# A hybrid encoder's feed-forward entry: differences by ScalarE and accumulating transfers, plain gates ahead of the second value block

## The chip, the core and the metric

One core of one Trainium2 chip runs the whole program. The metric is device time in microseconds (us) from the start of the program to its end; lower is better. Engines by the profile's names: PE (matrix products) and PEld (its weight loads), DVE (VectorE), ACT (ScalarE), POOL (GpSimd), SP (SyncE, which here only issues transfers).

## What is computed

Two layers of a streaming encoder over 656 token columns (528 of a prompt, 8 streams of 16). Each layer has an input projection, three head groups, an output projection, and then the gated feed-forward part that the change touches:

```python
h2 = rmsnorm(x, p['g_ffn'])
gate, val = jnp.split(h2 @ p['w_up'].astype(x.dtype), 2, axis=-1)
gate_c, ffn_new = causal_dwconv(gate, ffn_past, p['ffn_conv_w'], p['ffn_conv_b'])
x = x + (jax.nn.gelu(gate_c) * val) @ p['w_down'].astype(x.dtype)
```

Model width is 1024 (8 blocks of 128 rows), feed-forward width 2816: 22 gate blocks and 22 value blocks of 128. `causal_dwconv` is three taps along the columns; its state `ffn_past` fills two columns ahead of each stream.

## The kernel before

**Layout.** Activations lie transposed: 128 channels on the partitions, 656 columns along them. Each product is made three times from a rounded high part and a low remainder (`mm3`: hi times hi, hi times lo, lo times hi), so every weight and activation block is first split: ACT casts the high part (`whi`, `hi_h`, `fh`), DVE subtracts it for the low part (`wlo`, `lo_h`, `fh` again). The weight parts live in a ring of `NW = 4` buffers ("passing" ones, tiles whi and wlo, each half a block's depth), or, with `own=True`, in slots of their own (tiles ghi and glo).

**The feed-forward entry** is the stretch from the end of the output projection to the first Strassen products; there is one per layer (from about 397.8 and 1222.4 us). In order on PE: one group of products `e_u` for gates 0 and 1 and value 0 (`gemm_group`), value block 1 (`d_v`: two column halves, eight blocks deep, three products each, so 48), gate blocks 2 and 3 (`d_g`, 48 each; `NPG = 2`), then all remaining gate and value blocks in pairs by Strassen's seven products (`strassen`), each four blocks deep and one column half wide, so 12 instructions of PE; the first such products are value pair 0's (`d_v<-fh`).

**Right factors.** The Strassen products need seven combinations of the normalised input, which `factors` makes. It scales the eight x blocks (DVE, L1068), makes the differences t1 to t4 of halves on POOL (L1076, L1077, L1084, L1085: 16 subtractions of 128x328 in a layer), and splits each of the 7 x 4 results (ACT cast and DVE subtraction, L1090, tile fh). It is a generator with seven steps; step n needs `src[k][n]`. `FE = 2` steps are taken before the gates, the rest after.

**A plain gate** (`plain_gate`): `gate_in` puts the past columns into the tile gp by POOL (L1100, L1102), DVE evicts the products into gp with the norm's factor r (L1248), `gate_out` copies the new state into gout (POOL, L1107, L1108), then the taps run: ACT the first (L1112), DVE two more (L1115), ACT the gelu (L1118, after a table load). For value blocks 0 and 1, POOL multiplies the gate by r (L1257, L1258) and DVE multiplies the value product by it (gv, L1262 to L1264).

**What sets the order.** The program is written as one stream; each engine takes its instructions in the order printed below, and waits for others by semaphores. A DMA that POOL issues occupies POOL in that order. Weights come by SP's queue. Sums of Strassen's weight blocks are POOL's too (wcb, L985). Strassen's results are added up by DVE (L1018, L1022) as soon as each product is done, and the down projection (`d_dn`) begins once the first value pair is gated (POOL L1299) and split (hi_g, lo_g).

Of the kernel before, what the change touches and what calls it, by code (L numbers as in the profile page):

```python
# [13 lines left out]
ALU = mybir.AluOpType  # L14
# [23 lines left out]
NPG = 2  # L38
# [121 lines left out]
def trunk_kernel(ctx: ExitStack, tc: tile.TileContext, i: dict, o: dict, depth: int = 2):  # L160
# [12 lines left out]
    V, A, G, PE = nc.vector, nc.scalar, nc.gpsimd, nc.tensor  # L173

    def S(name, dt=F32):
        return slots.tile([128, T], dt, tag="S", name=name)
# [22 lines left out]
    xs = [S(f"x{m}") for m in range(8)]  # L199
# [25 lines left out]
    def par(name, k):  # L225
        c = COLS[name][0] + k
        return cst[:, c:c + 1]
# [136 lines left out]
    def w_load(w, k0, kt, parts=None):  # L364
        raw = wraw.tile([128, 8, 128], F32, tag="raw", name="raw")
        for a, b in parts or ((0, kt),):
            nc.sync.dma_start(out=raw[:, a:b], in_=w[:, (k0 + a) * 128:(k0 + b) * 128].rearrange("p (k n) -> p k n", n=128))
        return raw
# [4 lines left out]
    def w_split(raw, kt, a=0, own=False):  # L373

        half = 4 if kt in (4, 8) else 3
        units = []
        while a < kt:
            n = min(half, kt - a)
            if own:
                hi, lo = unit_s("ghi"), unit_s("glo")  # L380
            else:
                hi = wsp.tile([128, 4, 128], F32R, tag="whi", name="whi")
                lo = wsp.tile([128, 4, 128], F32R, tag="wlo", name="wlo")
            seq(A.copy(hi[:, :n], raw[:, a:a + n]))  # L384
            seq(V.tensor_tensor(out=lo[:, :n], in0=raw[:, a:a + n], in1=hi[:, :n].bitcast(F32), op=ALU.subtract))  # L385
            units += [(hi, lo, m) for m in range(n)]
            a += n
        return units

    def weights(w, k0, kt, own=False):  # L390
        return w_split(w_load(w, k0, kt), kt, 0, own)
# [8 lines left out]
    def gemm1(units, ks, rhs, nm, ab, P=PD):  # L400
        ps = P(f"d_{nm}")
        for k in range(len(ks)):
            mm3(ps, units[k], rhs[ks[k]], ab, k == 0, k == len(ks) - 1)
        return ps

    def gemm(units, ks, rhs, nm, cc=CA, P=PD):

        return [gemm1(units, ks, rhs, f"{c}_{nm}", cc[c], P) for c in range(2)]
# [652 lines left out]
    def factors(l, r, cc):  # L1061

        (a0, a1), (b0, b1) = cc
        w = a1 - a0
        src = []
        for k in range(4):
            for m in (k, k + 4):
                V.scalar_tensor_tensor(out=xs[m][:, a0:T], in0=xs[m][:, a0:T], scalar=par("g_ffn", 8 * l + m),  # L1068
                                       in1=r[:, a0:T], op0=ALU.mult, op1=ALU.mult)
            b11, b12 = xs[k][:, a0:a1], xs[k][:, b0:b1]  # L1070
            b21, b22 = xs[k + 4][:, a0:a1], xs[k + 4][:, b0:b1]
            t = S(f"ft{l}{k}")
            t1, t3 = t[:, :w], t[:, HC:HC + w]
            t = S(f"fu{l}{k}")
            t2, t4 = t[:, :w], t[:, HC:HC + w]
            G.tensor_tensor(out=t1, in0=b12, in1=b11, op=ALU.subtract)  # L1076
            G.tensor_tensor(out=t2, in0=b22, in1=t1, op=ALU.subtract)  # L1077
            src.append((b11, b21, t2, t3, t4, t1, b22))
        out = [[] for k in range(4)]
        for n in range(7):  # L1080
            for k in range(4):
                b11, b21, t2, t3, t4, t1, b22 = src[k]
                if n == 1:
                    G.tensor_tensor(out=t3, in0=b22, in1=xs[k][:, b0:b1], op=ALU.subtract)  # L1084
                    G.tensor_tensor(out=t4, in0=b21, in1=t2, op=ALU.subtract)  # L1085
                x = src[k][n]
                t = S(f"fh{l}{k}{n}", F32R)
                hi, lo = t[:, :w], t[:, HC:HC + w]
                A.copy(hi, x)
                V.tensor_tensor(out=lo, in0=x, in1=hi.bitcast(F32), op=ALU.subtract)  # L1090
                out[k].append((hi, lo))
            yield out
# [4 lines left out]
    def gate_in(l, ft, gpast, a0):  # L1097
        g = SE(f"gp{l}{ft}")
        if a0 == 0:
            G.memset(g[:, 0:2], 0.0)  # L1100
        gs = by_stream(g[:, 2 + TP:])
        G.tensor_copy(gs[:, :, 0:2], by_stream(gpast[:, ft]))  # L1102
        return g, gs
# [25 lines left out]
    def gate_dst(g, gs, cc):  # L1129
        (c0, c1), (d0, d1) = cc  # L1130
        n0 = TP - d0
        return [[(g[:, 2 + c0:2 + c1], 0, c1 - c0, same)],
                [(g[:, 2 + d0:2 + TP], 0, n0, same), (gs[:, :, 2:18], n0, n0 + 128, by_stream)]]


    ks8 = list(range(8))
    for l in range(depth):
# [7 lines left out]
        if l == 0:  # L1145
            hs = []
# [56 lines left out]
        cx, cy = (CB, CC) if l == depth - 1 else (CA, CA)  # L1203
# [19 lines left out]
        hs = []  # L1223
        wu = i["w_up"][l]
# [12 lines left out]
        wd = i["w_down"][l]  # L1237
        a0, cw = cy[0][0], cx[0][1] - cx[0][0]
        gates, vals, gts = {}, {}, {}
        fac = factors(l, r, cx)  # L1240
        for n in range(FE):
            tm = next(fac)

        def plain_gate(ft, ps):
            g, gs_ = gate_in(l, ft, gpast, a0)
            for c, dd in enumerate(gate_dst(g, gs_, cx)):
                for out, a, b, v in dd:
                    V.tensor_tensor(out=out, in0=v(ps[c][:, a:b]), in1=v(r[:, cx[c][0] + a:cx[c][0] + b]), op=ALU.mult)  # L1248
            gates[ft] = gate_out(l, ft, g, gs_, gout, a0)

        for ft in range(2):
            plain_gate(ft, ps3[ft])
        wg = [weights(wu[ft], 0, 8, True) for ft in range(2, 2 + NPG)]
        for ft in range(2):
            ps = ps3[2] if ft == 0 else gemm(weights(wu[NFF + 1], 0, 8), ks8, hs, f"v{l}1", cx, PB)
            a, av = gates.pop(ft)
# [6 lines left out]
            V.tensor_tensor(out=v[:, d0:TP], in0=ps[1][:, :n0], in1=a[:, d0:TP], op=ALU.mult)  # L1263
            V.tensor_tensor(out=by_stream(v[:, TP:T]), in0=by_stream(ps[1][:, n0:n0 + 128]), in1=av, op=ALU.mult)  # L1264

        for ft in range(2, 2 + NPG):
            plain_gate(ft, gemm(wg[ft - 2], ks8, hs, f"g{l}{ft}", cx))
        for tm in fac:
            pass

# [81 lines left out]
        for p in range(1, NFF // 2):  # L1352
            for up in (up_gate, up_val)[1 if p == 1 else 0:]:
                for st in up(p):
# [3 lines left out]
                    while due and due[0][0] <= nprod:  # L1358
                        _, n, j = due.pop(0)
# [33 lines left out]
        if l < depth - 1:  # L1393
            hs = []
# [95 lines left out]
```

## Time and profile before

| | before |
|---|---|
| time, median of 3 runs | 1680.81 us (1680.68 to 1682.55) |
| the profiled execution's own time | 1678.91 us |
| its span, first to last instruction | 1677.1 us |
| mean granted TensorE clock | 0.993 |
| PE, PEld busy | 1618.5 us (97%), 1527.1 us (91%) |
| DVE, ACT, POOL busy | 1245.9 us (74%), 879.1 us (52%), 566.8 us (34%) |
| transfers | 180.56 MB, mean 108 GB/s; POOL's queue 12672 packets, 29.37 MB |

The profiled execution ran 1.81 us outside its span and stands 1.90 us under the median of the runs. Busy times are sums over the span; the stretches that matter here are read below by windows and by single rows.

### The profile page before, as it was taken

The numbers are of one execution on the slowest core, as the hardware profiler recorded it, in microseconds if no ns is written. First come the engines' busy times: TensorE is split into PE (matmuls) and PEld (weight loads), VectorE is DVE, ScalarE is ACT, GpSimd is POOL, SyncE is SP. The second block draws the span as 40 slices with busy tenths as digits, with TensorE's granted clock in tenths as the row PEclk, the third lists the DMA queues.
The fourth block names the chain that finished last, engine by engine and source line by source line (L and its number), as shares of the span: only waits on it lengthen the run. The fifth ranks groups of instructions, "written<-read, shape, count | busy, mean of one in ns | idle before, by whom it ended". The sixth has DMA issues, their size and how long they took to land.

```text
span 1677.1 us, 28733 instructions
## 1 busy us (share of the span) xinstructions
PE 1618.5 (97%) x10774; PEld 1527.1 (91%) x10774; DVE 1245.9 (74%) x2391; ACT 879.1 (52%) x1744; POOL 566.8 (34%) x652
## 2 busy tenths in 40 slices
PE   7999999999899999999999999999999999999997
PEld 7898888898899999999998988888988899999997
DVE  6579985769987767666647898856899777777556
ACT  6656576543554444444437556566545444444444
POOL 0102220007556555554001032100276545554420
PEclk9999999999999999999999999999999999999999
DMA  6236441342144444444532364313511344444453
GB/s 226 74 95 160 111 105 36 113 136 99 45 119 102 102 106 106 105 106 112 190 103 81 95 149 98 99 56 130 179 39 51 98 105 102 102 106 99 108 136 122
DMA packets 75003, 180.56 MB, mean 108 GB/s; under 512 B 12752, under 2 KB 18384, under 8 KB 74864
## 3 DMA queue, kind: packets, MB, share of 16 engines
q1 hardware_dynamic: 62192, 149.36, 27.6%
q0 software_dynamic: 12672, 29.37, 11.2%
q8 instruction: 84, 1.38, 0.3%
q14 instruction: 55, 0.45, 0.1%
HBM read 129.80 MB, written 35.46 MB: 99 GB/s over the span
## 4 chain that ended last, share of the span: by engine, by line
PE 78%; DVE 11%; issue 4%; POOL 3%; ACT 2%; DMA 1%; SPq 0%; POOLq 0%; DVEq 0%; ACTq 0%
PE d_dn L398 16%; PE d_i L398 16%; PE d_v L398 12%; PE d_g L398 12%; PE d_oa L398 5%; PE sc L515 2%; PE e_i L398 1%; PE hl L809 1%; PE po L551 1%; DVE fh L1090 1%; DVE wlo L385 1%; PE d_fin L398 1%; PE e_u L398 1%; DVE wlo L992 1%; POOL gv L1299 1%
## 5 line engine op out<-in xcount | busy, mean ns | idle before, releaser
L398 PE MATMUL d_v<-fh,whi 128*128 128x328 f32 (+1 forms) x1120 | 251.8, 312 | 1.6 <-ACT whi L991 1.6
L384 ACT CAST whi<-raw 128x384 fp32r<-128x384 f32 (+2 forms) x243 | 132.6, 548 | 208.8 <-PE d_i L398 76.5
L398 PE MATMUL d_g<-fh,whi 128*128 128x328 f32 (+1 forms) x1008 | 226.5, 312 | 0.3 <-ACT whi L991 0.3
L398 PE MATMUL d_i<-hi_h,whi 128*128 128x328 f32 x672 | 219.3, 326 | 0.0
L398 PE MATMUL d_i<-lo_h,whi 128*128 128x328 f32 x672 | 213.9, 318 | 0.0
L398 PE MATMUL d_i<-hi_h,wlo 128*128 128x328 f32 x672 | 212.9, 317 | 0.0
L398 PE MATMUL d_dn<-hi_g,wlo 128*128 128x328 f32 (+1 forms) x640 | 199.8, 312 | 2.8 <-DVE wlo L385 2.8
L398 PE MATMUL d_dn<-hi_g,whi 128*128 128x328 f32 (+1 forms) x640 | 200.2, 313 | 1.9 <-ACT hi_g L356 1.7
L398 PE MATMUL d_dn<-lo_g,whi 128*128 128x328 f32 (+1 forms) x640 | 200.1, 313 | 1.8 <-DVE lo_g L357 1.8
L385 DVE TENSOR_TENSOR wlo<-raw,whi 128x384 fp32r<-128x384 f32 (+2 forms) x243 | 170.9, 717 | 30.5 <-ACT whi L384 22.7
L398 PEld LDWEIGHTS d_v<-fh,whi 128*128 128x128 f32 x1120 | 189.3, 189 | 2.2 <-ACT whi L991 2.2
L992 DVE TENSOR_TENSOR wlo<-wcb,whi 128x512 fp32r<-128x512 f32 x152 | 131.9, 868 | 74.9 <-ACT whi L991 72.3
L398 PE MATMUL d_v<-fh,wlo 128*128 128x328 f32 (+1 forms) x560 | 175.5, 313 | 3.3 <-DVE wlo L992 3.3
L398 PEld LDWEIGHTS d_g<-fh,whi 128*128 128x128 f32 x1008 | 170.4, 189 | 0.5 <-ACT whi L991 0.5
L398 PE MATMUL d_g<-fh,wlo 128*128 128x328 f32 (+1 forms) x504 | 157.8, 313 | 2.3 <-DVE wlo L992 2.3
L985 POOL TENSOR_TENSOR wcb<-raw 128x512 f32<-128x512 f32 x76 | 109.6, 1442 | 127.8 <-DMA raw<-in_w_up 80.2
L992 DVE TENSOR_TENSOR wlo<-raw,whi 128x512 fp32r<-128x512 f32 x114 | 114.8, 1008 | 50.7 <-ACT whi L991 50.5
L991 ACT CAST whi<-wcb 128x512 fp32r<-128x512 f32 x152 | 93.7, 620 | 110.6 <-PE d_g L398 33.3
L398 PEld LDWEIGHTS d_i<-hi_h,whi 128*128 128x128 f32 x672 | 127.5, 190 | 10.1 <-issue 5.6
L398 PEld LDWEIGHTS d_i<-lo_h,whi 128*128 128x128 f32 x672 | 127.6, 190 | 3.8 <-issue 1.3
L398 PEld LDWEIGHTS d_i<-hi_h,wlo 128*128 128x128 f32 x672 | 127.2, 189 | 3.0 <-issue 1.3
L398 PEld LDWEIGHTS d_dn<-hi_g,wlo 128*128 128x128 f32 x640 | 121.1, 189 | 3.5 <-DVE wlo L385 3.5
(394 smaller groups left out, 4026.9 us busy)
## 6 DMA issues: line engine op xcount, KB each, us to landing
raw<-in_w_up SPq DMA_DIRECT2D x88, 512.0 KB, 3.7
raw<-in_w_in SPq DMA_DIRECT2D x45, 512.0 KB, 3.7
raw<-in_w_down SPq DMA_DIRECT2D x48, 384.0 KB, 3.8
x_scr<-x SPq DMA_DIRECT2D x24, 328.0 KB, 3.2
x_scr<-dd POOLq DMA_DIRECT2D x24, 328.0 KB, 4.5
x<-x_scr SPq DMA_DIRECT2D x24, 328.0 KB, 4.4
x_scr<-dd POOLq DMA_DIRECT2D x24, 320.0 KB, 4.6
cvb<-cvt POOLq DMA_DIRECT2D x20, 328.0 KB, 5.0
```

What stands on the lines that cost most here:

```text
L384: seq(A.copy(hi[:, :n], raw[:, a:a + n]))
L385: seq(V.tensor_tensor(out=lo[:, :n], in0=raw[:, a:a + n], in1=hi[:, :n].bitcast(F32), op=ALU.subtract))
L398: PE.matmul(ps[:, :b - a], lhsT=ww[:, n], rhs=r[:, a:b], start=first and j == 0, stop=last and j == 2)
L515: PE.matmul(ps[:, o0:o0 + w], lhsT=q[64 * c:64 * c + 64, q0:q0 + 128], rhs=k[64 * c:64 * c + 64, n * w:(n + 1) * w], start=True, stop=True)
L551: PE.matmul(po[:, :128], lhsT=vt[:, j * 128:(j + 1) * 128], rhs=aT[:, j * 128:(j + 1) * 128], start=j == 0, stop=False)
L809: PE.matmul(ps[:, c * 128:(c + 1) * 128], lhsT=kk[:, 16 + 128 * c:144 + 128 * c], rhs=both(m0 + 64 * c, 64), start=True, stop=True)
L985: G.tensor_tensor(out=t, in0=x, in1=y, op=op)
L991: A.copy(hi, x)
L992: V.tensor_tensor(out=lo, in0=x, in1=hi.bitcast(F32), op=ALU.subtract)
L1090: V.tensor_tensor(out=lo, in0=x, in1=hi.bitcast(F32), op=ALU.subtract)
L1299: G.tensor_tensor(out=v[:, a0:TP], in0=v[:, a0:TP], in1=a[:, a0:TP], op=ALU.mult)
```

## The change

In `factors`, POOL's 16 subtractions of a layer go. For each k, ACT now writes four starting values: t3 = -b12 and t1 = -b11 (L1077, L1079), t2 = b11 (L1081), t4 = -b22 (L1082). POOL issues transfers that add to what lies at their destination: t3 += b22 (L1078), t1 += b12 (L1080), and in the new loop (L1086) t4 += b21, t2 += t3, t4 += t1. That is 16 ACT instructions and 20 transfers of 128x328 numbers (164 KB) in a layer. In the layer's code, the weights of gates 2 and 3 are loaded and split before `factors`, in the passing buffers and not in slots of their own, and both gates run before value block 1, with one step of `factors` taken ahead of each. The four casts and four subtractions of these weights now lie among the splits at the output projection's end; SP issues the same loads, the gates' one place earlier.

```diff
--- before.py
+++ after.py
@@ -1073,16 +1073,21 @@
             t1, t3 = t[:, :w], t[:, HC:HC + w]
             t = S(f"fu{l}{k}")
             t2, t4 = t[:, :w], t[:, HC:HC + w]
-            G.tensor_tensor(out=t1, in0=b12, in1=b11, op=ALU.subtract)
-            G.tensor_tensor(out=t2, in0=b22, in1=t1, op=ALU.subtract)
+
+            A.mul(t3, b12, -1.0)
+            G.dma_start(out=t3, in_=b22, accum_op=ALU.add)
+            A.mul(t1, b11, -1.0)
+            G.dma_start(out=t1, in_=b12, accum_op=ALU.add)
+            A.copy(t2, b11)
+            A.mul(t4, b22, -1.0)
             src.append((b11, b21, t2, t3, t4, t1, b22))
+        for n, m in ((4, 1), (2, 3), (4, 5)):
+            for s in src:
+                G.dma_start(out=s[n], in_=s[m], accum_op=ALU.add)
         out = [[] for k in range(4)]
         for n in range(7):
             for k in range(4):
                 b11, b21, t2, t3, t4, t1, b22 = src[k]
-                if n == 1:
-                    G.tensor_tensor(out=t3, in0=b22, in1=xs[k][:, b0:b1], op=ALU.subtract)
-                    G.tensor_tensor(out=t4, in0=b21, in1=t2, op=ALU.subtract)
                 x = src[k][n]
                 t = S(f"fh{l}{k}{n}", F32R)
                 hi, lo = t[:, :w], t[:, HC:HC + w]
@@ -1237,6 +1242,7 @@
         wd = i["w_down"][l]
         a0, cw = cy[0][0], cx[0][1] - cx[0][0]
         gates, vals, gts = {}, {}, {}
+        wg = [weights(wu[ft], 0, 8) for ft in range(2, 2 + NPG)]
         fac = factors(l, r, cx)
         for n in range(FE):
             tm = next(fac)
@@ -1250,7 +1256,9 @@
 
         for ft in range(2):
             plain_gate(ft, ps3[ft])
-        wg = [weights(wu[ft], 0, 8, True) for ft in range(2, 2 + NPG)]
+        for ft in range(2, 2 + NPG):
+            next(fac)
+            plain_gate(ft, gemm(wg[ft - 2], ks8, hs, f"g{l}{ft}", cx))
         for ft in range(2):
             ps = ps3[2] if ft == 0 else gemm(weights(wu[NFF + 1], 0, 8), ks8, hs, f"v{l}1", cx, PB)
             a, av = gates.pop(ft)
@@ -1263,8 +1271,6 @@
             V.tensor_tensor(out=v[:, d0:TP], in0=ps[1][:, :n0], in1=a[:, d0:TP], op=ALU.mult)
             V.tensor_tensor(out=by_stream(v[:, TP:T]), in0=by_stream(ps[1][:, n0:n0 + 128]), in1=av, op=ALU.mult)
 
-        for ft in range(2, 2 + NPG):
-            plain_gate(ft, gemm(wg[ft - 2], ks8, hs, f"g{l}{ft}", cx))
         for tm in fac:
             pass
 
```

What this makes of POOL's order in the first layer's entry. Before (ft and fu hold t1, t3 and t2, t4; x are the scaled blocks; gp the gates' tiles):

```order
L1076 TENSOR_TENSOR ft_4493<-x_3460 128x328
L1077 TENSOR_TENSOR fu_4494<-x_3850,ft_4493 128x328
L1084 TENSOR_TENSOR ft_4493<-x_3850,x_3460 128x328
L1085 TENSOR_TENSOR fu_4494<-x_3850,fu_4494 128x328
...
L1084 TENSOR_TENSOR ft_4511<-x_4006,x_3798 128x328
L1085 TENSOR_TENSOR fu_4512<-x_4006,fu_4512 128x328
L1107 COPY gout_4490<-gp_4547 128x2
L1108 COPY gout_4490<-gp_4547 128x16
L1100 MEMSET gp_4560 128x2
L1102 COPY gp_4560<-gpast_4062 128x8x2
L1107 COPY gout_4490<-gp_4560 128x2
```

After:

```order
L985 TENSOR_TENSOR wcb<-raw 128x512
L1078 DMA ft_4513<-x_3850 128x328
L1080 DMA ft_4513<-x_3460 128x328
L1086 DMA fu_4514<-x_3850 128x328
...
L1086 DMA fu_4524<-x_3902 128x328
L1086 DMA fu_4514<-ft_4513 128x328
...
L1086 DMA fu_4534<-ft_4533 128x328
L1086 DMA fu_4544<-ft_4543 128x328
L1112 COPY gout_4490<-gp_4587 128x2
L1113 COPY gout_4490<-gp_4587 128x16
L1105 MEMSET gp_4600 128x2
L1107 COPY gp_4600<-gpast_4062 128x8x2
```

The four POOL instructions of each k are now five transfers, partly gathered at the train's end; the state copies of gates 0 and 1 (gp_4587 and gp_4600, before gp_4547 and gp_4560) still stand right behind the whole train.

On DVE, after the evictions of the e_u group. Before:

```order
L1248 TENSOR_TENSOR gp_4560<-e_u_4343,r_h_4327 128x8x16
L1115 SCALAR_TENSOR_TENSOR ga_4555<-gp_4547,cst,ga_4555 128x672
L385 TENSOR_TENSOR glo<-raw,ghi 128x512
L1115 SCALAR_TENSOR_TENSOR ga_4555<-gp_4547,cst,ga_4555 128x672
L1115 SCALAR_TENSOR_TENSOR ga_4568<-gp_4560,cst,ga_4568 128x672
L385 TENSOR_TENSOR glo<-raw,ghi 128x512
L1115 SCALAR_TENSOR_TENSOR ga_4568<-gp_4560,cst,ga_4568 128x672
L385 TENSOR_TENSOR glo<-raw,ghi 128x512 x2
L1262 TENSOR_TENSOR gv_4595<-e_u_4344,ga_4555 128x328
L1263 TENSOR_TENSOR gv_4595<-e_u_4345,ga_4555 128x200
L1264 TENSOR_TENSOR gv_4595<-e_u_4345,ga_4555 128x128
L1262 TENSOR_TENSOR gv_4661<-d_v_4609,ga_4568 128x328
```

After:

```order
L1254 TENSOR_TENSOR gp_4600<-e_u_4343,r_h_4327 128x8x16
L1120 SCALAR_TENSOR_TENSOR ga_4595<-gp_4587,cst,ga_4595 128x672
L1095 TENSOR_TENSOR fh_4613<-fu_4514,fh_4613 128x328
L1120 SCALAR_TENSOR_TENSOR ga_4595<-gp_4587,cst,ga_4595 128x672
L1120 SCALAR_TENSOR_TENSOR ga_4608<-gp_4600,cst,ga_4608 128x672
L1095 TENSOR_TENSOR fh_4616<-fu_4524,fh_4616 128x328
...
L1254 TENSOR_TENSOR gp_4675<-d_g_4625,r_h_4327 128x328
...
L1270 TENSOR_TENSOR gv_4765<-e_u_4344,ga_4595 128x328
...
L1272 TENSOR_TENSOR gv_4765<-e_u_4345,ga_4595 128x128
L385 TENSOR_TENSOR wlo<-raw,whi 128x512
L1120 SCALAR_TENSOR_TENSOR ga_4683<-gp_4675,cst,ga_4683 128x672
```

The glo subtractions are gone from here; the low parts fh of steps 2 and 3 and the eviction of gate 2's first half (gp_4675<-d_g_4625) now stand behind the taps of gate 1 (ga_4608), and value 1's low weights (L385 wlo) behind value 0's gating (gv_4765).

On ACT, from gate 3's taps to the weights of the third and fourth Strassen products. Before:

```order
L384 CAST ghi<-raw 128x512
L991 CAST whi<-wcb 128x512 x2
L1089 CAST fh_4791<-fu_4494 128x328
L1089 CAST fh_4794<-fu_4500 128x328
L1089 CAST fh_4797<-fu_4506 128x328
...
L1089 CAST fh_4827<-ft_4493 128x328
L1089 CAST fh_4830<-ft_4499 128x328
L1112 ACTIVATE ga_4723<-gp_4715,cst 128x672
L1089 CAST fh_4833<-ft_4505 128x328
```

After:

```order
L1123 ACTIVATE ga_4683<-ga_4683 128x672
L991 CAST whi<-raw 128x512 x2
L1117 ACTIVATE ga_4758<-gp_4750,cst 128x672
L1123 ACTIVATE ga_4758<-ga_4758 128x672
L1094 CAST fh_4835<-fu_4514 128x328
L1094 CAST fh_4838<-fu_4524 128x328
...
L1094 CAST fh_4865<-x_3954 128x328
L1094 CAST fh_4868<-x_4006 128x328
L991 CAST whi<-wcb 128x512 x2
```

The casts whi<-wcb (Strassen's third and fourth weights) stood ahead of all the casts fh of the later steps; they now stand behind gate 3's gelu (ga_4758) and twelve casts fh.

## Rows read from the trace of the kernel before

**Rows 1.** The profile's first part: busy time, share and instructions of each engine.

```profile
PE 1618.5 (97%) x10774; PEld 1527.1 (91%) x10774; DVE 1245.9 (74%) x2391; ACT 879.1 (52%) x1744; POOL 566.8 (34%) x652
```

**Rows 2.** Timeline, PE, first entry: start, us, operation, [idle before, releaser].

```profile
411.49 0.32 PE L398 MATMUL d_v<-hi_h,whi 128*128 128x328 f32 x1
...
419.60 0.39 PE L398 MATMUL d_g<-hi_h,ghi 128*128 128x328 f32 x1 [0.74 <-DVE gp L1248]
422.56 0.64 PE L398 MATMUL d_g<-hi_h,glo 128*128 128x328 f32 x1 [2.41 <-DVE glo L385]
...
446.99 0.57 PE L398 MATMUL d_v<-fh,whi 128*128 128x328 f32 x2 [1.39 <-ACT whi L991]
448.03 0.42 PE L398 MATMUL d_v<-fh,wlo 128*128 128x328 f32 x1 [0.48 <-DVE wlo L992]
454.30 0.42 PE L398 MATMUL d_g<-fh,wlo 128*128 128x328 f32 x1 [0.37 <-DVE wlo L992]
```

**Rows 3.** Waits, 410 to 470 us: us in total, times, longest.

```profile
PE d_dn L398 <- DVE lo_g L357: 1.8, 2, 1.0
```

**Rows 4.** Windows: us; busy (instructions) PE, PEld, DVE, ACT, POOL; PE's clock; DMA share; GB/s.

```profile
420.00:424.00 4.00, 1.59 (x6) 1.45 (x6) 3.86 (x7) 3.78 (x5) 2.56 (x9) 0.80 0.00 0
424.00:428.00 4.00, 4.00 (x23) 4.00 (x22) 3.26 (x6) 3.52 (x7) 3.28 (x2) 0.78 0.41 131
```

**Rows 5.** Timeline, POOL, both entries.

```profile
400.69 1.49 POOL L1076 TENSOR_TENSOR ft<-x 128x328 f32<-128x328 f32 x1
...
419.75 0.88 POOL L1085 TENSOR_TENSOR fu<-x,fu 128x328 f32<-128x328 f32 x1
...
420.88 0.20 POOL L1102 COPY gp<-gpast 128x16 f32<-128x16 f32 x1
...
424.72 2.68 POOL L1257 TENSOR_TENSOR ga<-ga,r_h 128x528 f32<-128x528 f32 x1 [2.16 <-ACT ga L1118]
...
428.21 1.33 POOL L1257 TENSOR_TENSOR ga<-ga,r_h 128x528 f32<-128x528 f32 x1
...
1225.31 1.33 POOL L1076 TENSOR_TENSOR ft<-x 128x322 f32<-128x322 f32 x1
...
1243.03 0.86 POOL L1085 TENSOR_TENSOR fu<-x,fu 128x322 f32<-128x322 f32 x1
```

**Rows 6.** Transfers that POOL issues at L725: summary (ns min/median/max) and timeline, POOL.

```profile
L725 POOL DMA_DIRECT2D cvb<-cvt x20: 845/864/1850, 121.0 to 1047.1; - x20
DMA to landing us min/median/max: 3.6/4.6/7.3
...
142.43 1.84 POOL L725 DMA_DIRECT2D cvd<-cvt  x2
...
151.78 0.87 POOL L725 DMA_DIRECT2D cvd<-cvt  x1
152.34 1.38 POOL L903 TENSOR_TENSOR hvx<-hvt,cst 128x512 f32<-128x512 f32 x1
```

**Rows 7.** Timeline, DVE.

```profile
142.35 0.83 DVE L672 TENSOR_TENSOR oh<-oh,r_on 128x656 f32<-128x656 f32 x1
...
397.77 12.38 DVE L1068 SCALAR_TENSOR_TENSOR x<-x,cst,r_h 128x656 f32<-128x656 f32 x8
410.07 8.97 DVE L1090 TENSOR_TENSOR fh<-x,fh 128x328 fp32r<-128x328 f32 x8
...
430.46 1.72 DVE L1090 TENSOR_TENSOR fh<-fu,fh 128x328 fp32r<-128x328 f32 x4
...
447.30 0.68 DVE L992 TENSOR_TENSOR wlo<-raw,whi 128x512 fp32r<-128x512 f32 x1
...
457.34 0.49 DVE L1018 TENSOR_TENSOR gv<-d_v,us_v 128x328 f32<-128x328 f32 x1
```

**Rows 8.** Timeline, ACT.

```profile
421.11 0.95 ACT L1112 ACTIVATE ga<-gp,cst 128x672 f32<-128x672 f32 x1 [0.19 <-POOL gp L1102]
...
427.86 1.56 ACT L1089 CAST fh<-fu 128x328 fp32r<-128x328 f32 x4
```

## The prediction

> **What bounds the kernel now.** The busy times come first [rows 1]: PE is busy 97% of the span, so the kernel is PE's work plus PE's waits, and a change that leaves the number of PE instructions as it is can only win back waits, or time at a lower clock. The timeline of PE in the first entry shows them [rows 2]: after the e_u group ends at 411.49, PE waits 0.74 + 2.41 us at gate 2, 1.39 + 0.48 us at the fifth Strassen product and 0.37 us once more, 5.39 us in all; the waits' view adds 1.8 us at the first down products [rows 3]. Behind the gate-2 waits the granted clock is 0.80 and 0.78 for two stretches of 4 us, and 1.00 outside them [rows 4]: 0.20 x 4 + 0.22 x 4 = 1.7 us, half level (1.2 GHz) for part of each. So one entry holds about 8.9 us that are not work, two entries some 18 us, and the most that this change could touch is that.
>
> Who ends those waits? DVE. Its timeline [rows 7] shows the eight scalings at 12.38 / 8 = 1.55 us and the eight first fh at 8.97 / 8 = 1.12 us, one behind another to 418.97; POOL's differences run beside them from 400.69 to 420.63 [rows 5]. Away from them an operation of the same size takes 0.83 us (128x656) and 1.72 / 4 = 0.43 us (128x328) [rows 7]. And right behind POOL's train stand the state copies that the second gate's taps need: the last of them before gate 1's first tap is at 420.88 [rows 5], and ACT starts that tap at 421.11, 0.19 us after it was free [rows 8].
>
> **What the change costs and brings, part by part.**
>
> *ACT's 16 starting values per entry.* Each is a 128x328 instruction; the nearest row is 1.56 / 4 = 0.39 us for casts of that size [rows 8]; 16 x 0.39 = 6.2 us. ACT is busy 52% [rows 1] and before was waiting for DVE's scalings there, so on the path lies only one of them, ahead of the first transfer, beside POOL's last weight sum (which ends at 400.69 [rows 5]): 0. Without that cover it would be 0.4 us per entry. The gates' weight casts moved into the output projection's end are the same number, on engines that do as much there before: 0, at most one low part of 0.68 us [rows 7] per entry.
>
> *POOL's 20 transfers.* The 16 subtractions took 420.63 - 400.69 = 19.94 us. What an accumulating transfer costs POOL no row shows. The nearest rows are plain transfers issued at L725 [rows 6]: 0.845 to 1.85 us, median 0.864; two back to back take 1.84, so 0.92 from start to start; a subtraction behind one began 152.34 - 151.78 = 0.56 us after its start. The bounds are 20 x 0.56 = 11.2 us and 20 x 1.85 = 37 us; I take 0.92, the back-to-back row, because this is a back-to-back train: 18.4 us. It starts when the first pair is scaled. Two contended scalings take 2 x 1.55 = 3.1 us from 397.77, and POOL's weight sums still run then, so about 401.2; the train ends at 419.6, 1.0 us before the subtractions' end. In the second entry POOL starts at 1225.31 and the subtractions end at 1243.89 [rows 5], so 1225.4 + 18.4 = 1243.8: no gain. The train is barely shorter than what it replaces.
>
> *DVE's relief.* With no subtractions beside them, 8 x (1.55 - 0.83) + 8 x (1.12 - 0.43) = 11.3 us per entry come off DVE. This is the large number, and I give it almost no weight: DVE's queue then has gate 1's taps (ga_4608), and these wait for the state copies behind POOL's train. Behind that waiting tap stand fh of steps 2 and 3 and the eviction of gate 2's first half, so DVE finishes early and then idles.
>
> *The new chain of the first entry.* State copies end at about 420.0 (train 419.6, three copies 0.4). ACT's tap 0.95: 420.9. DVE: tap 0.83, fh 0.43, tap 0.83, two fh 0.86, eviction 0.43, in all 3.4: gate 2's buffer is free at 424.3. PE has done e_u and three halves of gates by 411.5 + 3 x 3.6 = 422.3 (24 instructions of 0.15 us a half, by the spacing of PE's rows at full clock): **it waits 2.0 us**. Its fourth half ends at 427.9. Value 1's low weights stand on DVE behind value 0's gating, which waits for ACT's gelu and POOL's product with r. Before, POOL's product began 424.72 - 421.08 = 3.6 us after the copy; now that comes to 423.6 plus some 1.1 us of casts moved ahead, 424.7; POOL takes 1.33 to 2.68 us and a second piece [rows 5], DVE some 1.1 for value 0 and 0.68 for the weights: 428.5 to 430.3, I take 430: **it waits 2.1 us**. Value 1 (7.2) and two Strassen products (3.6) bring PE to 440.8. The third product's weights are cast behind gate 3's gelu and twelve fh. That gelu needs gate 3's evictions and taps, which DVE makes behind two pairs of low weights, to about 438.5; 12 x 0.39 and the cast: 443.4, **2.6 us of wait**; the low weights stand on DVE behind the same twelve low parts (12 x 0.43) and value 1's gating, to 445.1: **1.3 us more**. That is 8.0 us of waits. From there DVE runs without a break: two more low weights (2 x 0.6) than stood before in the stretch from 447.30 to 457.75, one tap (0.83) fewer, and one or two weight sums of POOL that now fall into it and cost DVE up to 0.7 us each. The stretch before was 10.45 us, so 444.5 + 1.2 + 10.45 - 0.83 gives 455.3, and with the sums 456.7. The last eviction of value pair 0 [rows 7] ended at 457.75 before. The down projection's first waits (1.8 us) hang on it, and they are where the gain is paid out: **-1.1 us**, from the late end, since by the early end PE itself would be the later of the two.
>
> *Clock.* The waits of 2.0 and 2.1 us may bring the clock down as 0.74 + 2.41 did; each fall costs about 1.7 us of products [rows 4]. But the third product waits for ACT and DVE, not PE, so such a loss shortens the 3.9 us of wait there: 0.
>
> Second entry: by the same chain with a train that ends where the subtractions did, 0.
>
> Sum: -1.1 + 0 = -1.1 us against the profiled execution's 1678.91: 1677.8. That execution stands 1.9 us under the runs' median, so against the median: 1680.81 - 1.1 = **1679.7 us**. About 0.2% (3.4 us) is what a measurement of this kernel can tell from no change; this forecast lies within it.
>
> **The rivals.**
>
> *Faster: the transfers go out more quickly than 0.92 us.* All of DVE's 11.3 us of relief wait behind the train, so each 0.01 us of spacing is worth 20 x 0.01 x 2 = 0.4 us over both entries. For it: single issues took 0.864 us, and work behind one began after 0.56. At 0.80 the gain is 4.8 us: 1674.9. At 0.56 the train would end 7 us earlier and PE's waits at the gates vanish, but no more than about 6.5 us per entry can be had: 1666.7. Faster by 0.2% needs 0.86 us or less. Against it: both pairs in the rows are at 0.92.
>
> *Slower: the train stretches.* Above 0.92 + 4.5 / 40 = 1.03 us per transfer the kernel ends slower by 0.2%; at 1.08 it takes 1680.81 - 1.1 + 6.4 = 1686.1. For it: the longest issue at L725 took 1.85. Against it: two issues at 142.43 ran beside a DVE operation with two inputs, and neither was slowed (0.92 and 0.83 us) [rows 6, 7]. The Trainium skill (SBUF — State Buffer, "The 'DVE blocks DMA' trap") says that POOL cannot write a transfer's descriptors while DVE runs an operation in a two-port mode; by it the train would wait for such operations. Its section "Who interferes with whom" says that tensor_tensor has no such mode, and in this stretch DVE runs only that and scalar_tensor_tensor; the trace's 0.92 beside L672 agrees.
>
> *Slower: the transfers land late.* POOL takes the train in order, and t2 += t3 of the last k is issued five places (4.6 us) behind the transfer that finishes t3. Plain ones land in 3.6 to 7.3 us, median 4.6 [rows 6]; adding to the destination may take longer. Landings above 4.6 us stop POOL, and the state copies behind it, by the excess: at 6.9 us, 2.3 us in each entry, 1684.3; at 7.3, 1685.1.
>
> **Chances.** My forecast 0.48 (0.07 of it over the bound to faster, 0.03 to slower), faster transfers 0.25 (0.22 over the bound), stretched train 0.12 (0.10), late landings 0.15 (0.11): faster 0.29, slower 0.24, same 0.47. The range runs from 1674.0 (spacing 0.78) to 1686.5 (spacing 1.09); it leaves out about 0.1 of faster trains and 0.08 of slower ones.
>
> **What would show it.** In the changed kernel's profile: 40 transfers at L1078, L1080 and L1086 at 0.92 us spacing; the state copy of gate 1 near 420; the scalings near 0.83 and the first fh near 0.43 for all but the first two or three; DVE then idle until that copy; PE waiting about 2 us at gate 3 for gp (L1254), about 2 us at value 1 for wlo (L385), about 4 us at the third Strassen product; POOL some 38 us (the subtractions, 19.9 + 18.6) and DVE some 23 us (2 x 11.3) less busy. I am wrong if the train is much shorter or longer than 18.4 us, if gate 1's taps don't wait for it, or if PE's waits in an entry sum to something other than about 8 us.

## The result: slower, and the profile after

The changed kernel takes 1691.23 us (median of 6 runs, 1688.64 to 1693.19) against 1681.49 us for the kernel before in the same session (6 runs): a ratio of 1.0055 (of the means), with a 95% interval from 1.0041 to 1.0070. That is 9.7 us more, where 1.1 us less was forecast, and above the range's upper end of 1686.5. Its profiled execution has a span of 1687.1 us, 10.0 us over the 1677.1 us of before.

The first part of the profile after, and the line of POOL's queue in its third part (packets, MB, share of 16 DMA engines):

```profile
PE 1621.6 (96%) x10774; PEld 1533.3 (91%) x10774; DVE 1223.2 (73%) x2391; ACT 891.5 (53%) x1776; POOL 560.5 (33%) x660
...
q0 software_dynamic: 18432, 36.02, 13.9%
```

DVE is 22.7 us less busy than in [rows 1], as forecast (23 us), and the kernel is slower all the same. POOL saves only 6.3 us, not 38, since the issues count as work (40 x 0.87 = 34.8 us). Timeline of POOL in the first entry, after:

```profile
401.32 0.89 POOL L1078 DMA_DIRECT2D ft<-x  x1 [2.25 <-PE e_u L398]
401.95 1.17 POOL L1080 DMA_DIRECT2D ft<-x  x1
402.55 1.47 POOL L1086 DMA_DIRECT2D fu<-x  x1
404.52 0.88 POOL L1078 DMA_DIRECT2D ft<-x  x1 [0.49 <-ACT fu L1081]
405.64 0.86 POOL L1080 DMA_DIRECT2D ft<-x  x1 [0.25 <-ACT ft L1079]
...
412.57 0.88 POOL L1078 DMA_DIRECT2D ft<-x  x1 [0.29 <-ACT ga L1117]
413.74 0.87 POOL L1080 DMA_DIRECT2D ft<-x  x1 [0.29 <-issue]
...
423.72 0.86 POOL L1086 DMA_DIRECT2D fu<-ft  x1 [0.26 <-issue]
424.55 0.52 POOL L1107 COPY gp<-gpast 128x16 f32<-128x16 f32 x1
```

The first transfer goes out at 401.32 (401.2 was said). The first three follow at 0.6 us, their records overlapping. From 404.52 on each row takes POOL 0.86 to 0.88 us, and POOL then stands still for about 0.3 us: 404.52 to 413.74 is 8 steps of 1.15. The train ends at 424.58, so 20 transfers took 23.3 us, 1.16 each, and gate 1's state copy starts at 424.55 where it had started at 420.88 [rows 5].

What holds the transfers back can be seen in the windows of the same entry (columns as in [rows 4]):

```profile
404.00:408.00 4.00, 4.00 (x29) 4.00 (x28) 2.75 (x6) 3.90 (x11) 2.68 (x5) 1.00 0.97 151
408.00:412.00 4.00, 4.00 (x29) 4.00 (x28) 3.84 (x12) 2.12 (x6) 3.13 (x4) 1.00 0.91 139
...
428.00:432.00 4.00, 2.47 (x9) 2.47 (x10) 3.67 (x8) 3.99 (x7) 2.33 (x2) 0.50 0.00 0
432.00:436.00 4.00, 4.00 (x19) 4.00 (x18) 4.00 (x10) 0.95 (x1) 4.00 (x7) 0.60 0.00 0
```

POOL is busy 2.7 to 3.1 of each 4 us; the sixteen DMA engines are busy 0.91 to 0.97 of it, at 139 to 151 GB/s. Then DVE, after:

```profile
397.95 7.51 DVE L1068 SCALAR_TENSOR_TENSOR x<-x,cst,r_h 128x656 f32<-128x656 f32 x8
406.71 3.37 DVE L1095 TENSOR_TENSOR fh<-x,fh 128x328 fp32r<-128x328 f32 x8 [1.25 <-ACT fh L1094]
...
426.08 0.92 DVE L1120 SCALAR_TENSOR_TENSOR ga<-gp,cst,ga 128x672 f32<-128x672 f32 x1 [11.44 <-ACT ga L1117]
...
428.98 0.50 DVE L1254 TENSOR_TENSOR gp<-d_g,r_h 128x328 f32<-128x328 f32 x1
```

The scalings fell from 1.55 us [rows 7] to 7.51 / 8 = 0.94, the first fh from 1.12 to 0.42; and all of it is given back in one wait of 11.44 us for gate 1's tap, which stands behind the state copy. The eviction that frees PE's buffer ends at 429.5. PE, after, both entries:

```profile
429.53 0.64 PE L398 MATMUL d_g<-hi_h,whi 128*128 128x328 f32 x1 [6.90 <-DVE gp L1254]
...
448.14 0.57 PE L398 MATMUL d_v<-fh,whi 128*128 128x328 f32 x2 [1.36 <-ACT whi L991]
449.71 0.42 PE L398 MATMUL d_v<-fh,wlo 128*128 128x328 f32 x1 [1.00 <-DVE wlo L992]
...
1257.19 0.63 PE L398 MATMUL d_g<-hi_h,whi 128*128 128x322 f32 x1 [7.80 <-DVE gp L1254]
1275.53 0.56 PE L398 MATMUL d_v<-fh,whi 128*128 128x322 f32 x2 [2.01 <-ACT whi L991]
1277.06 0.41 PE L398 MATMUL d_v<-fh,wlo 128*128 128x322 f32 x1 [0.97 <-DVE wlo L992]
```

In the first entry that is 6.90 + 1.36 + 1.00 = 9.26 us of waits where [rows 2] have 5.39, and behind the 6.90 us PE runs at a granted clock of 0.50 and 0.60, at and near its 1.2 GHz level. The 24 products behind it take 6.44 us:

```profile
429.53 6.44 PE d_g L398 x24
```

At 0.15 us each they would take 3.6, so the clock costs 2.8 us; behind the 2.41 us wait of before it cost at most 1.7 [rows 4].

Measured from the last product of the output projection's first half (d_oa) to the first of the down projection (d_dn), the first entry is 4.9 us longer than before and the second 6.6 us. Of the first, 0.6 us lie ahead of e_u's last product, 4.6 between that and the first Strassen product, where the wait is 3.75 us longer (6.90 against 0.74 + 2.41) and the clock costs 1.1 more, and 0.4 are won back behind. Outside the entries the program is 1.5 us shorter. The two entries are the whole loss.

### The profile page after: what moved, and what is told of

The parts are those of the page before. It is cut to its first block, busy times and chain, and to the rows that moved or that the text cites. A ratio compares the mean times of both kernels' runs of the same rounds, so it can differ in the third digit from the quotient of the medians.

```text
span 1687.1 us, 28833 instructions
## 1 busy us (share of the span) xinstructions
PE 1621.6 (96%) x10774; PEld 1533.3 (91%) x10774; DVE 1223.2 (73%) x2391; ACT 891.5 (53%) x1776; POOL 560.5 (33%) x660
## 3 DMA queue, kind: packets, MB, share of 16 engines
q0 software_dynamic: 18432, 36.02, 13.9%
## 4 chain that ended last, share of the span: by engine, by line
PE 79%; DVE 10%; issue 3%; ACT 3%; POOL 2%; DMA 1%; SPq 0%; POOLq 0%; DVEq 0%; ACTq 0%
PE d_dn L398 17%; PE d_i L398 16%; PE d_g L398 13%; PE d_v L398 13%; PE d_oa L398 5%; PE e_i L398 2%; PE sc L515 2%; PE hl L809 1%; PE po L551 1%; DVE wlo L385 1%; PE d_fin L398 1%; POOL fu L1086 1%; DVE ga L1120 1%; DVE x L1068 1%; DVE lo_h L360 1%
## 5 line engine op out<-in xcount | busy, mean ns | idle before, releaser
L384 ACT CAST whi<-raw 128x384 fp32r<-128x384 f32 (+2 forms) x251 | 137.4, 550 | 211.9 <-PE d_i L398 76.1
L385 DVE TENSOR_TENSOR wlo<-raw,whi 128x384 fp32r<-128x384 f32 (+2 forms) x251 | 177.9, 723 | 30.2 <-ACT whi L384 20.2
L985 POOL TENSOR_TENSOR wcb<-raw 128x512 f32<-128x512 f32 x76 | 113.9, 1499 | 121.5 <-DMA raw<-in_w_up 84.1
```

The source lines that it names most:

```text
L985: G.tensor_tensor(out=t, in0=x, in1=y, op=op)
```

## The experiments

Theory A is that the entry's time goes with the length of POOL's train, because the state copies, through them gate 1's taps, and through these PE's buffers stand behind it. Rivals: the new order of the gates, or the passing weight buffers, cost the time; or the time is bound by DVE. What all runs gave ("entries": first and second, against before, measured as above in the profiled execution; outside the entries such differences come to 4 us at most, so single microseconds in them mean little; the ratio is that of the means; number 9's profiled execution is the longest of its five, 1669.67 us):

| kernel | us (runs) | before | ratio, interval | entries |
|---|---|---|---|---|
| changed | 1691.23 (6) | 1681.49 | 1.0055, 1.0041 to 1.0070 | +4.9, +6.6 |
| 1 state copies first | 1687.49 (4) | 1680.61 | 1.0041, 1.0026 to 1.0056 | +5.6, +3.5 |
| 2 new order alone | 1685.56 (9) | 1680.61 | 1.0030, 1.0016 to 1.0044 | +1.9, +1.9 |
| 3 transfers alone | 1690.57 (4) | 1680.61 | 1.0058, 1.0043 to 1.0073 | +3.6, +6.0 |
| 4 half transfers | 1685.14 (10) | 1680.61 | 1.0022, 1.0012 to 1.0032 | +2.7, +2.6 |
| 5 copying everywhere | 1667.05 (1) | 1679.55 | none | -5.0, -3.4 |
| 6 before, copies first | 1680.58 (10) | 1679.55 | 0.9999, 0.9988 to 1.0011 | -0.8, +0.7 |
| 7 late transfers | 1684.21 (5) | 1679.55 | 1.0031, 1.0019 to 1.0043 | +1.2, +2.5 |
| 8 late subtractions | 1683.22 (12) | 1679.55 | 1.0021, 1.0010 to 1.0032 | +1.8, +1.7 |
| 9 split train, new order | 1667.49 (5) | 1680.34 | 0.9929, 0.9916 to 0.9942 | -4.8, -4.2 |
| 10 split train, old order | 1676.59 (11) | 1680.34 | 0.9980, 0.9971 to 0.9989 | -3.7, -1.1 |
| 11 copying, old order | 1666.11 (4) | 1680.34 | 0.9919, 0.9905 to 0.9933 | -6.6, -4.1 |
| 12 copying in the entry alone | 1671.51 (4) | 1679.06 | 0.9948, 0.9932 to 0.9965 | -5.6, -2.3 |

**1. State copies ahead of the train.**

```diff
         wg = [weights(wu[ft], 0, 8) for ft in range(2, 2 + NPG)]
+        ready = {ft: gate_in(l, ft, gpast, a0) for ft in range(2)}
         fac = factors(l, r, cx)
...
-            g, gs_ = gate_in(l, ft, gpast, a0)
+            g, gs_ = ready[ft] if ft < 2 else gate_in(l, ft, gpast, a0)
```

> Edit: in the changed kernel the two state copies of gates 0 and 1 are made ahead of the transfer train, all else as it is. Theory A (the train itself bounds PE: gate 1's taps wait for the state copy behind 20 transfers, and gate 2's eviction stands behind those taps on DVE): PE's wait at gate 3 falls from 6.9 and 7.8 us to 1.5 to 3 us, since the cast of t2's second block still stands ahead of gate 1's tap on ACT; the clock falls less; total 1678 to 1684 us. Rival B (the fh casts that wait for the transfers' landing are what holds the queue, the copy is only late with them): the wait stays above 5 us and the total above 1687.

1687.49 us. The long wait at gate 3 is gone, as theory A has it, but little of the time is, so neither expectation is met. PE in the first entry:

```profile
426.51 0.42 PE L398 MATMUL d_g<-hi_h,whi 128*128 128x328 f32 x1 [1.91 <-DVE gp L1255]
433.70 0.42 PE L398 MATMUL d_v<-hi_h,wlo 128*128 128x328 f32 x1 [1.45 <-DVE wlo L385]
...
447.25 0.56 PE L398 MATMUL d_v<-fh,whi 128*128 128x328 f32 x2 [2.76 <-ACT whi L991]
448.82 0.64 PE L398 MATMUL d_v<-fh,wlo 128*128 128x328 f32 x1 [1.00 <-DVE wlo L992]
```

These are the four waits of the prediction's chain, which had 2.0, 2.1, 2.6 and 1.3 us, and the clock falls after two of them (0.62 in the 4 us from 428, 0.51 in those from 448). So the copies were only the first of several things late behind the train: POOL's product of the gate with r is behind it too, and so are the factors that DVE and ACT split.

**2 and 3. The two halves of the change apart.** Number 2 has the gates' new order and the passing weight buffers with POOL's old subtractions; number 3 is the kernel before with `factors` as the change has it.

```diff
-            A.mul(t3, b12, -1.0)
-            G.dma_start(out=t3, in_=b22, accum_op=ALU.add)
...
+            G.tensor_tensor(out=t1, in0=b12, in1=b11, op=ALU.subtract)
+            G.tensor_tensor(out=t2, in0=b22, in1=t1, op=ALU.subtract)
...
```

> Edit: only the new order of gates and the passing weight buffers; the differences are POOL's 16 subtractions as before. Theory A: the subtractions end where they did (about 20 us after the first), so PE's wait at gate 3 is 2 to 4 us and the total 1679 to 1685. Rival C (the order of gates itself costs, since value block 1 no longer covers the time until gate 1's taps): total 1687 or more with subtractions too.

> Edit: only the differences by ScalarE and accumulating transfers; order of gates and own weight slots as before. Theory A: the state copy comes about 4 us later than before the change (23 us of train in place of 20), the low weights of gate 2 stand behind gate 1's tap on DVE, so PE's wait for them grows from 2.4 to 5 to 7 us: total 1686 to 1692. Rival C (the order of gates costs): total 1678 to 1683.

1685.56 and 1690.57 us. The transfers alone give the whole loss: PE, number 3:

```profile
427.45 0.64 PE L398 MATMUL d_g<-hi_h,ghi 128*128 128x328 f32 x1 [6.45 <-ACT ghi L384]
```

In the old order the 6.45 us come at gate 2, for a weight cast behind the tap on ACT; the tap waits for the state copy, here at 425.39. The new order alone costs some 5 us as well, for another reason:

```profile
419.26 0.64 PE L398 MATMUL d_g<-hi_h,whi 128*128 128x328 f32 x1 [6.82 <-DVE gp L1249]
```

This is gate 2's first product, right behind e_u, and not gate 3, for which 2 to 4 us had been expected. It needs a PSUM buffer (where PE puts its results) that DVE, slowed by the subtractions, has not read yet (it starts on e_u's results at 418.72); before, value block 1 had its own pool and filled that time. The two costs don't add up (1.0030 and 1.0058 against 1.0055 together): with the transfers DVE starts on e_u's results at 410.00, and this wait is gone.

**4. Half the columns in each transfer.**

```diff
-            G.dma_start(out=t3, in_=b22, accum_op=ALU.add)
+            G.dma_start(out=t3[:, :w // 2], in_=b22[:, :w // 2], accum_op=ALU.add)
...
```

> Edit: each of the 40 accumulating transfers covers only half its columns (82 KB in place of 164); half of the differences is left out. Theory T1 (the DMA engines take 1.15 us for an accumulating transfer of 164 KB, 145 GB/s, and POOL is held back to that rate): spacing falls to about 0.9 us, the train to about 18 us, total 1677 to 1684. Theory T2 (issuing an accumulating transfer costs POOL 1.15 us whatever its size): spacing stays 1.1 to 1.2, total 1689 to 1693.

1685.14 us, just above the 1684 that T1 allows. Timeline of POOL:

```profile
404.90 0.88 POOL L1078 DMA_DIRECT2D ft<-x  x1
405.82 0.86 POOL L1080 DMA_DIRECT2D ft<-x  x1
406.73 0.86 POOL L1086 DMA_DIRECT2D fu<-x  x1
```

An issue takes as long as at full size, but the pauses between these issues are gone: 0.92 us from start to start, and 0.98 over the whole train (402.13 to 421.80). PE's wait at gate 3 falls to 3.34 us. So at full size the bytes set the rate, not POOL.

**5, 11 and 12. Copying instead of adding.** In number 5 `accum_op=ALU.add` is taken off every transfer of the changed kernel, those of the convolution (L725) and of the down projection (L1336) included; number 11 does the same in the old order of the gates; number 12 takes it off the entry's 20 alone.

```diff
-            G.dma_start(out=t3, in_=b22, accum_op=ALU.add)
+            G.dma_start(out=t3, in_=b22)
...
```

> Edit: the changed kernel with the 40 transfers as plain copies of the same size (they overwrite in place of adding, so the differences are not formed). Theory T1a (the addition is what makes 164 KB take 1.15 us on the DMA engines): spacing falls to 0.9 us, train to about 18 us, as with half the size. Theory T1b (any transfer of 164 KB between these tiles takes 1.15 us of the engines, adding or not): spacing stays 1.1 to 1.2 us and the train 22 to 24.

> Edit: the differences by ScalarE and plain transfers of full size (they overwrite, the differences are not formed), with the old order of gates; the counterpart of e5. If the new order of gates gains once the train is short (about 12 us, as in e5): this is 3 us or more above e5's 1667.05, 1670 to 1677. If the gain of e5 is the train's alone: 1665 to 1669.

> The changed kernel with only the 20 transfers of each entry (L1078, L1080, L1086) copying instead of adding: the differences are not formed, so the output is not the reference's. The two earlier kernels with copying transfers had taken the addition off the transfers at L725 and L1336 as well; this one leaves those adding, as in the kernel before. Theory A (the gain is that of the entry's 12-us train alone): the time stays within 3 us of 1667.05, that is 1664 to 1670, with the two entries (end of the output projection to the first down product) together some 8.5 to 10.5 us shorter than before, and the outside of them within 1.5 us of before. Rival (a part of the gain came from the transfers of the convolution and of the down projection): entries as in the earlier kernel, but 3 us or more of the gain are gone: 1670 to 1674. Spacing of the entry's transfers 0.60 us by both; L725 back at 0.86 us by both.

1667.05, 1666.11 and 1671.51 us. The summaries of L1086 in number 12, and of L725 in number 5 (ns min/median/max):

```profile
L1086 POOL DMA_DIRECT2D fu<-ft x16: 538/538/547, 406.8 to 1236.1; - x16
```

```profile
L725 POOL DMA_DIRECT2D cvb<-cvt x20: 536/537/730, 120.9 to 1039.1; - x20
```

Without the addition an issue takes 0.54 us, the first train of number 12 goes from 403.24 to 415.06 at 0.59 us each (number 5's at 0.60, shorter than either of its theories had it), and PE has no wait at the gates. Number 12 falls into its rival's band (1670 to 1674): its entries give 7.9 us, 0.6 short of what theory A expected of them, and the outside of them nothing. So some 5 of the 12.5 us that number 5 gained in its one run come from the other transfers, in which alone the two kernels differ. Numbers 5 and 11 differ by no more than a microsecond: with a short train the order of the gates makes no difference that the one run of number 5 can show.

**6. The kernel before with its state copies first** (the edit of number 1 on it).

> Edit: the kernel before the change with the state copies of gates 0 and 1 made ahead of POOL's subtractions, all else as it was. Theory A' (before the change too the copies behind POOL's train end the entry's first wait): 1676 to 1679 us. Rival D (there the contended DVE ends it: eight scalings and eight fh run until 419, whatever POOL copies): within 2 us of 1680.6.

1680.58 us, no difference. In the kernel before the copies were not what came last: DVE, slowed by the subtractions, was.

**7 and 8. Some of the differences later.** POOL forms t3 = b22 - b12 and t2 = t3 + b11 first; t1 and t4 follow behind gate 1's state copy, by adding transfers (7) or by subtractions (8).

```diff
...
+            if n == 2:
+                for k in range(4):
+                    b11, b21, t2, t3, t4, t1, b22 = src[k]
+                    A.mul(t1, b11, -1.0)
+                    A.mul(t4, t2, -1.0)
+                    with tc.issue_after(start["copy"]):
+                        G.dma_start(out=t1, in_=xs[k][:, b0:b1], accum_op=ALU.add)
+                        G.dma_start(out=t4, in_=b21, accum_op=ALU.add)
...
```

> Edit: the kernel before the change, with only t3 and t2 (needed first) by POOL subtractions and additions, 8 in an entry; t1 and t4 (needed late) by ScalarE and 8 accumulating transfers, issued behind gate 1's state copy. Order of gates as before. Theory A (train length ahead of the copies, and contention of DVE beside it, bound the entry): POOL's work ahead of the copies is halved to about 10.5 us, the first fh end at about 415 in place of 419, the waits at gate 2 (0.74 + 2.41 us) and the clock fall behind them go: 1672 to 1678 us. Rival E (DVE's later queue up to the eviction at 457.75 bounds it and takes the gain back): 1679 to 1682.

> Edit: as e7, but t1 and t4 are POOL subtractions as before, only issued behind gate 1's state copy. Theory A: the gain of e7 less what contention costs later, as POOL's subtractions now run beside DVE's taps and low weights: 1674 to 1680. Rival E: 1680 to 1684.

1684.21 and 1683.22 us, both slower: a miss for theory A, with number 7 above its rival's band too. The waits of number 7 from 400 to 470 us (in total, times, longest):

```profile
POOL gout L1114 <- DVE gp L1255: 8.4, 2, 4.4
...
DVE gv L1269 <- POOL ga L1264: 6.1, 2, 5.4
...
PE d_g L398 <- DVE gp L1255: 4.4, 1, 4.4
```

DVE waits 5.4 us at once for POOL's product with r, which has come behind the late half of the work. Moving work on POOL past the state copies alone moves the wait to the next thing that POOL owes.

**9 and 10. A split train.** The eight transfers of the factors used first (t3, then t2) stay ahead; the other eight come behind, t4 as -t2 + b21 by ACT, and only once gate 1's tap is issued. 16 transfers are left of 20, and the state copies of gates 0 and 1 come first.

```diff
...
+        for s in src:
+            last = G.dma_start(out=s[2], in_=s[3], accum_op=ALU.add)
...
+            if n == 4:
+                with tc.issue_after(start["tap"]):
+                    for s in src:
+                        A.mul(s[4], s[2], -1.0)
+                with tc.issue_after(last.ins):
+                    for k in range(4):
+                        G.dma_start(out=src[k][5], in_=xs[k][:, b0:b1], accum_op=ALU.add)
+                    for s in src:
+                        G.dma_start(out=s[4], in_=s[1], accum_op=ALU.add)
...
```

> Edit: the changed kernel's order of gates, with the train cut in two: 8 accumulating transfers (t3 += b22, t2 += t3) first, then 8 more (t1 += b12, t4 = -t2 by ScalarE and t4 += b21, in place of 12), and the state copies of gates 0 and 1 made ahead of all. Theory A (what stands ahead of gate 1's tap and of t2's landing is the cost): t2 lands near 415, PE's wait at gate 3 falls below 1 us, the clock falls once at most in an entry: 1666 to 1674 us. Rival F (two or three short waits remain at value 1's weights and at the third Strassen product, as in e1, and each brings the clock down): 1680 to 1688.

> Edit: the same split train and early state copies, with the old order of gates and their own weight slots. Theory A: DVE is free of contention, gates 2 and 3 find their buffers and low weights ready, the waits of 0.74 + 2.41 us and the clock fall go: 1670 to 1677. Rival E (DVE's queue up to the eviction at 457.75 takes it back): 1679 to 1684.

1667.49 us with the new order of the gates: 0.7% faster than the kernel before, with everything computed. DVE and then PE in its first entry:

```profile
416.82 0.49 DVE L1263 TENSOR_TENSOR gp<-d_g,r_h 128x328 f32<-128x328 f32 x1
```

```profile
438.75 0.57 PE L398 MATMUL d_v<-fh,whi 128*128 128x328 f32 x2 [1.36 <-ACT whi L991]
...
440.31 0.42 PE L398 MATMUL d_v<-fh,wlo 128*128 128x328 f32 x1 [0.99 <-DVE wlo L992]
```

The eviction for gate 3 starts 12.2 us earlier than in the changed kernel (428.98), PE has no wait between e_u and the third Strassen product, and its clock is 1.00 from 424 to 452 us. How much of this is the split, how much the four transfers fewer and the copies' place (some 3 us in number 1) was not run apart. With the old order the same train gives 1676.59 us, no more than 0.2% faster. There all of POOL's late transfers stand ahead of its product with r, where in number 9 four come behind it (DVE, number 10):

```profile
427.08 0.50 DVE L1276 TENSOR_TENSOR gv<-e_u,ga 128x328 f32<-128x328 f32 x1 [3.87 <-POOL ga L1271]
```

That this wait costs the 9 us is not shown: PE has no wait at the gates in number 10 either, its entries make up 4.2 us of the difference, and the rest lies outside them. So the gates' new order is worth 9 us once the train is split, nothing that shows with a 12-us train or with the full one, and less than nothing with the subtractions.

## Why the prediction was wrong, step by step

**The step that failed** is "I take 0.92, the back-to-back row, because this is a back-to-back train". It was 1.16 (1.18 in the second entry), the train 23.3 us and not 18.4. Three mistakes lie in it.

First, the transfers at L725 are called plain. They are not: line 725 ends in `accum_op=ALU.add`, and number 5 shows what a plain one takes there, 0.54 us against 0.864 [rows 6]. So the row was of the very operation, and 0.56, the low bound, is the pace of a copying train (0.59); an adding one keeps it for three issues only.

Second, the row is of no back-to-back pair: the next transfer of the pair waited for ACT, which makes its source. Number 5 shows it, where an issue is shorter, POOL stands still, and the pair is 0.92 apart all the same:

```profile
142.33 0.54 POOL L725 DMA_DIRECT2D cvd<-cvt  x1 [0.23 <-ACT cvt L723]
143.25 0.54 POOL L725 DMA_DIRECT2D cvd<-cvt  x1 [0.39 <-ACT cvt L723]
```

The closest pair of the kernel before went out 0.54 us apart (178.11 and 178.65). So 0.92 was neither what an issue costs nor what a transfer needs; that 1.16 lies only 26% above it is chance.

Third, the row holds POOL's issue of single transfers and pairs, and not what the DMA engines need. The first three issues of the train still go out at 0.6 us; only from the fourth on is POOL held back. The Trainium skill (Perfetto Trace Analysis, "DMA Instruction — SWDGE (GPSIMD)") says that the profiled end of such an instruction is the last written descriptor, not the last moved byte; the trace agrees, with issues of 0.86 us and landings 3.2 us (median) after their start. The price stood in the third part of the page of before, POOL's queue:

```profile
q0 software_dynamic: 12672, 29.37, 11.2%
```

11.2% of 1677.1 us is 187.8 us of all sixteen engines for 88 adding transfers of 320 to 328 KB (40 at L725, and 48 at L1330, which go to HBM), 2.13 us each; by its bytes, one of 164 KB takes 1.07 us, as an estimate. That is over 0.92 and over the 1.03 from which the prediction itself has the kernel slower. At 1.07 its own price gives 1679.7 + 0.15 x 40 = 1685.7 us. After the change the train's window in the first entry holds nothing but its 20 transfers (121 GB/s x 28 us is their 3.4 MB):

```profile
400.00:428.00 28.00, 22.63 (x151) 22.36 (x149) 14.66 (x27) 13.72 (x33) 18.41 (x28) 0.95 0.78 121
```

0.78 x 28 / 20 = 1.09 us of the engines for each, in steps of 1.16.

**The rival "the train stretches"** is what happened, at a chance of 0.12. Its price comes out: at 1.16 and 1.18 it gives -1.1 + 20 x (0.24 + 0.26) = +8.9 us against +9.7 measured. The wait shows it by itself: the first train was 4.9 us longer than said, and PE waited 6.90 us where 2.0 was said. That the sum comes so near is in part luck: the three waits behind gate 3 came to 2.4 us where 6.0 were said, and in the same entry the clock and the weights' casts, both put at nothing, took 3.4. Its evidence was of the wrong kind: it asked whether DVE's operations lengthen an issue. They don't, at 0.86 to 0.89 us beside the scalings and first fh (the first three take 2.70 us together); what stretches is the pause behind the issue. And the range stopped at a spacing of 1.09, though the sum's own bound was 1.85.

**The rival "faster"** is right in its mechanism and too dear: at 0.56 it has 1666.7, 14 us below before; number 12, at 0.59, gains 7.5. It took 6.5 us per entry to be had; with no wait left at the gates, the two entries gave 5.6 and 2.3.

**The rival "late landings"** is refuted: 2.9 to 4.7 us, median 3.2, where 4.6 was the limit. Pauses of 0.72 and 0.96 us in the first train and one of 1.83 in the second are the longest that could be of this kind, and they cost little: at 1.15 a step the trains would take 23.0 us, and they took 23.3 and 23.6.

**Chain of the first entry.** Right: the relief of DVE is worth nothing, since it stands still behind the state copy (11.44 us), and from the copy's end (425.1) to the eviction's it takes 4.4 us (4.3 said). The waits behind gate 3 were right for number 1, and shorter after the long wait: none at value 1, then 1.36 and 1.00.

**"Clock: 0"** is the other step that failed. It counted on later waits to absorb the fall. In the first entry the fall cost 2.8 us against the 1.7 of before; in the second, where the clock had stayed at 1.00, it fell twice:

```profile
1256.00:1260.00 4.00, 2.81 (x10) 2.81 (x11) 3.65 (x7) 3.66 (x7) 2.64 (x3) 0.50 0.00 0
1260.00:1264.00 4.00, 4.00 (x25) 4.00 (x25) 4.00 (x10) 0.94 (x1) 3.66 (x5) 0.84 0.00 0
...
1276.00:1280.00 4.00, 3.03 (x16) 2.94 (x16) 4.00 (x8) 2.60 (x6) 2.23 (x2) 0.79 0.00 0
1280.00:1284.00 4.00, 4.00 (x23) 4.00 (x23) 4.00 (x5) 1.48 (x4) 3.92 (x3) 0.78 0.77 262
```

By PE's busy time in them that is 3.6 us. Number 1 shows that the step fails by itself. It has nearly the waits that were said, and is 6.9 us slower than before; the second of its two falls comes behind the very waits that were to absorb the first:

```profile
428.00:432.00 4.00, 4.00 (x19) 3.98 (x18) 3.66 (x3) 1.72 (x4) 2.92 (x4) 0.62 0.03 3
...
448.00:452.00 4.00, 3.18 (x12) 3.18 (x13) 3.70 (x7) 1.99 (x5) 2.47 (x2) 0.51 0.00 0
452.00:456.00 4.00, 4.00 (x19) 4.00 (x19) 4.00 (x5) 1.62 (x3) 3.92 (x3) 0.63 0.59 197
```

Together they cost 4.6 us in that entry. Number 4 says the same: at a spacing of 0.98 the prediction's price gives 1.4 us more than before, and the kernel takes 4.5 more (2.0 to 5.4 by its interval).

**"The gates' weight casts: 0, at most 0.68 per entry"** is nearly right. In the first entry of every kernel of the new order PE waits 2.1 us for DVE's x (L441) in the output projection, against 1.6 in those of the old order; in the changed kernel e_u's last product comes 0.6 us later than before, counted from the last d_oa, and 0.2 us in the second entry.

**"Second entry: 0"** is wrong by 6.6 us, by the same spacing and the clock.

## What to carry to other kernels

A row of an issuing instruction says what the issuer pays; for a train of transfers also work out what the DMA engines need, from the queue's share of the span and its bytes, and take the larger. Before taking a spacing for a rate, look at what fed the pair. Before pricing a transfer by a row, read in the source whether that row copies or adds. When a freed engine stands behind a queue that became longer, split the queue by who needs what first: eight transfers ahead and eight behind, in place of 20 ahead, with the state copies first, turned 0.6% slower into 0.7% faster. And price the clock behind every wait: 1.91 us of waiting in number 1 were followed by 4 us at 0.62.

## What was not expected of the hardware

An adding transfer of 164 KB within SBUF costs more than a copying one twice over: 0.86 against 0.54 us of POOL, and 1.09 against 0.48 us of the DMA engines (number 12: a DMA share of 0.40 from 400 to 424 us, 9.6 us for 20). It is cut into 144 packets against 48, by the queue's counts (18432, 14592 and 12672). In the same 4 us the copying train of number 12 moves 282 GB/s at 0.80 of the engines, where the adding one has 139 at 0.91:

```profile
408.00:412.00 4.00, 4.00 (x29) 4.00 (x28) 3.37 (x9) 3.54 (x10) 3.52 (x7) 1.00 0.80 282
```

Half the bytes need 0.70 us (number 4: 0.58 of the same 24 us), more than half of 1.09, so a part of the price goes by transfer and not by byte. The Trainium skill (DMA: Bandwidth & Descriptors, "Anatomy of one DMA — SWDGE (gpsimd) path") has 2.0 us plus the bytes over 436 GB/s for one transfer, by estimate 2.4 us here; the copying ones of number 12 land after 2.4 us in the median, which agrees, and the adding ones after 3.2, where the measurement decides.
